# Strassen's seven products for a sample of two chunks, and prompt and sample in separate stages

## The chip, the cores and the metric

The kernel runs on one core of a Trainium2 chip. The metric is the device time of that core for one execution, in microseconds (us). The engines are named as the profile names them: PE is TensorE, which makes the matrix products, PEld its weight loads, DVE is VectorE, ACT is ScalarE, POOL is GpSimd, SP is SyncE, which issues the transfers. SBUF is the core's on-chip memory; PSUM is the memory into which PE writes.

## The reference

The program is a small encoder trunk of two layers with a width of 1024. It runs with the same weights on a prompt of 512 tokens and a sample of 1024 tokens. The core of it:

```python
for i in range(DEPTH):
    hn = rmsnorm(h, ln1[i])
    z = hn @ w_in[i]                        # 1024 -> 4352 columns
    q, k, v, ga, uf, gf, mga, mgf = jnp.split(z, SPLIT_IDX, axis=-1)
    ...
    a = band_attention(q, k, v, sink[i]) * jax.nn.silu(ga)
    f = fourier_mix(uf, w_fmix[i]) * jax.nn.silu(gf)
    merged = jax.nn.sigmoid(mga) * (a @ w_ao[i]) + jax.nn.sigmoid(mgf) * (f @ w_fo[i])
    h = h + merged @ w_out[i]
    gate = jax.nn.sigmoid(rmsnorm(h, ln_pg[i]) @ w_pg[i])
    h = h + (p[i].astype(h.dtype) @ w_pe[i]) * gate
return rmsnorm(h, ln_f)
```

`rmsnorm(x, g)` divides each token by the root of the mean of its squares and multiplies each channel by `g`. All of it is in float32.

## The kernel before

**Layout.** Channels lie on the 128 partitions and tokens on the free dimension. The 1536 tokens are three chunks of 512: chunk 0 is the prompt, chunks 1 and 2 are the sample. A width of 1024 is eight tiles k of 128 channels.

**Products.** A product of a 128x128 weight tile with a 128x512 activation tile is made in three passes: each operand is the exact sum of a hi and a lo half (`hi_lo`, L77: ACT casts to hi on L79, another engine subtracts to get lo on L80), and `mm3_steps` (L87) issues hi by hi (L91), hi by lo (L92) and lo by hi (L93). A result tile of 128 channels of one chunk has 8 k x 3 = 24 matmuls of 512 columns. `load_w` (L139) fetches a weight tile of eight k and splits it, ACT and POOL; the tile serves all three chunks, one after the other.

**Stages.** For each layer, `project` (L209) makes 34 tiles of the input projection for the three chunks. Beside it `run` interleaves, at so many steps per step of the projection, the input embedding's product, the attention (24 units: a block of 128 queries and one kv head), the Fourier mixing of the prompt and of the sample, and the first splits for the merge. Then `merge` (L301) has no second flow: both branches' projections with their gates, the output projection, and the gate's products (`w_pg`), each for eight tiles and three chunks. The residual h stays in SBUF through `merge`.

**Norm.** A token's scale is known only when all eight tiles of that token's h are there. `Norm.add` squares a tile on ACT and adds it on POOL (L182, L183); `stats` sums over partitions with tiny matmuls on PE (L188) and finds the reciprocal root with twelve tiny DVE operations (L190 to L197); `scale` spreads it over the partitions by transposes on PE (L203) and a copy (L205), and the result is the tile rb. The products do not wait for this: `split` (L165) puts only the channel's gain on a product's input, and rb is put on the product's output by DVE (`scaled`, L229; L354; for the rotary tables L249):

```python
def split(h, gain, k):
    t = big([P, 2, T], F32R)
    g = ln_sb[:, gain, k : k + 1]
    S.activation(t[:, 0, :], h, AF.Copy, scale=g)
    V.scalar_tensor_tensor(t[:, 1, :], h, g, f(t[:, 0, :]), op0=ALU.mult, op1=ALU.subtract)
```

**What sets the order.** The code is written for a tile framework: tiles come from pools with a fixed number of buffers (`BUFS`; PSUM has the tags mm, sc, o and misc with two banks each), the framework puts in the semaphores, and its scheduler puts each engine's instructions into an order when the program is built. At run time every engine works through its own list in that order.

## Time and profile before

| | |
|---|---|
| median of 3 runs | 2346.46 us (2344.33 to 2347.04) |
| the profiled execution, its span | 2344.3 us |
| mean granted TensorE clock | 0.988 |
| busy: PE, DVE, ACT, POOL | 97%, 51%, 34%, 28% |
| moved by DMA | 308.01 MB, 131 GB/s |

The span runs from the first to the last instruction of the profiled execution, which is one of its own beside the timed runs. In a row of the windows stand the stretch and its length, then busy time and number of instructions of PE, PEld, DVE, ACT and POOL, the granted clock (1.00 is full), the DMA engines' busy share and GB/s. A row of the timeline has start, duration, engine, line, operation, output and inputs by the program's names, and in brackets the idle time before it with what ended it. A row of the groups has the number of instructions, the busy sum, the mean ns of one, and the idle time before them. A matmul's duration is modelled and overlaps the next one.

### The profile page before, as it was taken

To read this page: it belongs to the slowest core of one execution; us is meant where nothing else is said; L and a number is where in the kernel's file an instruction comes from. 1 tells how busy PE (TensorE), PEld (TensorE's weight loads), DVE (VectorE), ACT (ScalarE), POOL (GpSimd) and SP (SyncE) were. 2 spreads that over 40 slices of the span, in tenths; PEclk is the share of its full clock that TensorE was granted. 3 is DMA by queue.
4 is the path that set the end of the run, shared out by engine and by line. 5 is a ranking of instruction groups with operands and counts; after the bars stand their busy time and mean duration, and the time that the engine had idled before them with its cause. 6 is when DMAs were issued, how large, how long until landed. Compare 5 with 4: busy or idle time off the path is not lost. (4 is left out here: it accounts for less than half of the span.)

```text
span 2344.3 us, 29343 instructions
## 1 busy us (share of the span) xinstructions
PE 2275.7 (97%) x10596; PEld 1885.0 (80%) x10596; DVE 1201.6 (51%) x2587; ACT 789.0 (34%) x1594; POOL 658.2 (28%) x427
## 2 busy tenths in 40 slices
...
GB/s 178 171 198 115 139 138 133 128 116 118 122 148 173 182 135 63 90 61 144 117 148 140 186 126 131 129 137 127 117 108 131 153 220 135 104 77 90 69 124 136
DMA packets 191905, 308.01 MB, mean 131 GB/s; under 512 B 15504, under 2 KB 89360, under 8 KB 191760
## 3 DMA queue, kind: packets, MB, share of 16 engines
...
HBM read 202.27 MB, written 103.81 MB: 131 GB/s over the span
## 5 line engine op out<-in xcount | busy, mean ns | idle before, releaser
L91 PE MATMUL mm<-act,wsp 128*128 128x512 f32 x1952 | 778.0, 399 | 2.6 <-DVE scr L222 2.6
L92 PE MATMUL mm<-act,wsp 128*128 128x512 f32 x1952 | 763.8, 391 | 1.2 <-DVE act L169 1.2
L93 PE MATMUL mm<-act,wsp 128*128 128x512 f32 x1952 | 763.4, 391 | 0.0
L80 POOL TENSOR_TENSOR wsp<-raw,wsp 128x1024 fp32r<-128x1024 f32 (+2 forms) x125 | 293.6, 2349 | 821.4 <-ACT wsp L79 671.2
L93 PEld LDWEIGHTS mm<-act,wsp 128*128 128x128 f32 x1952 | 366.8, 188 | 78.7
L91 PEld LDWEIGHTS mm<-act,wsp 128*128 128x128 f32 x1952 | 367.7, 188 | 69.9 <-issue 3.0
L92 PEld LDWEIGHTS mm<-act,wsp 128*128 128x128 f32 x1952 | 367.9, 188 | 69.3 <-DVE act L169 2.4
L79 ACT CAST wsp<-raw 128x1024 fp32r<-128x1024 f32 (+2 forms) x134 | 131.5, 986 | 427.0 <-PE mm L93 368.7
L229 DVE TENSOR_TENSOR scr<-mm,rb 128x512 f32<-128x512 f32 x170 | 117.3, 690 | 219.5 <-PE mm L93 218.2
L183 POOL TENSOR_TENSOR acc<-acc,scr 128x512 f32<-128x512 f32 x94 | 128.5, 1367 | 241.7 <-ACT scr L182 236.1
L501 ACT ACTIVATE act<-act,stat 128x384 f32<-128x384 f32 (+1 forms) x192 | 110.0, 574 | 199.4 <-DVE stat L499 198.5
L91 PE MATMUL sc<-act,wsp 128*128 128x512 f32 x416 | 165.9, 399 | 8.5 <-ACT act L168 8.5
L93 PE MATMUL sc<-act,wsp 128*128 128x512 f32 x416 | 165.2, 397 | 2.0 <-POOL wsp L80 2.0
L92 PE MATMUL sc<-act,wsp 128*128 128x512 f32 x416 | 165.7, 398 | 0.0
L91 PE MATMUL o<-act,wsp 128*128 128x512 f32 x416 | 163.2, 392 | 0.0
L92 PE MATMUL o<-act,wsp 128*128 128x512 f32 x416 | 162.6, 391 | 0.2 <-DVE act L169 0.2
L93 PE MATMUL o<-act,wsp 128*128 128x512 f32 x416 | 162.6, 391 | 0.0
L496 DVE CUSTOM_DVE_ANT_0 act<-sc,mask_sb 128x384 f32<-128x384 f32 (+1 forms) x192 | 91.1, 509 | 104.0 <-PE sc L491 103.5
L182 ACT ACTIVATE scr<-act 128x512 f32<-128x512 f32 x105 | 64.4, 628 | 227.6 <-DVE act L341 120.1
L80 DVE TENSOR_TENSOR act<-act,act 128x512 fp32r<-128x512 f32 (+1 forms) x144 | 113.3, 831 | 44.0 <-ACT act L79 40.6
L80 DVE TENSOR_TENSOR act<-misc,act 128x512 fp32r<-128x512 f32 x136 | 90.6, 686 | 52.0 <-ACT act L79 51.4
L323 POOL TENSOR_TENSOR act<-scr,scr 128x512 f32<-128x512 f32 x48 | 64.8, 1351 | 169.4 <-DVE scr L320 169.4
...
## 6 DMA issues: line engine op xcount, KB each, us to landing
...
gt<-scr SPq DMA_DIRECT2D x96, 256.0 KB, 2.0
scr<-gt SPq DMA_DIRECT2D x96, 256.0 KB, 2.8
q<-act SPq DMA_DIRECT2D x48, 256.0 KB, 3.2
gu<-scr SPq DMA_DIRECT2D x48, 256.0 KB, 2.2
pl<-scr SPq DMA_DIRECT2D x48, 256.0 KB, 2.2
...
```

Source lines behind the costliest of these rows:

```text
L79: S.copy(hi, src)
L80: lo_eng.tensor_tensor(lo, src, f(hi), op=ALU.subtract)
L91: PE.matmul(out, wh, xh, start=i == 0, stop=False)
L92: PE.matmul(out, wh, xl, start=False, stop=False)
L93: PE.matmul(out, wl, xh, start=False, stop=i == n - 1)
L182: S.activation(sq, h, AF.Square)
L183: eng.tensor_tensor(self.acc, self.acc, sq, op=ALU.add)
L229: V.tensor_tensor(a, out, rbs[c], op=ALU.mult)
L323: G.tensor_tensor(merged[c][-1][:, m % 2, :], ga, gf, op=ALU.add)
L496: V.tensor_tensor_reduce(out=pr, in0=sc[:, :W], in1=msk, scale=1.0, scalar=-3.0e38, op0=ALU.add, op1=ALU.max, accum_out=mx[:, e])
L501: S.activation(pr, pr, AF.Exp, bias=nmx[:, e], scale=0.125, accum_out=rs[:, e])
```

## The change

**Strassen's product.** For the sample, two weight tiles (m and m', 128 columns each), the two halves of the inner dimension (k 0 to 3, and 4 to 7) and the two chunks make a 2x2 by 2x2 block product. In place of eight half products of 4 k x 3 = 12 matmuls there are seven, in the form of Winograd with few sums. Class `Pair` holds it: four sums of weights on POOL, seven splits of weight halves (ACT, and POOL and DVE in turn), the seven products in three PSUM banks, and their combination by DVE and a copy by ACT. `pair_parts` makes the other side: for each k of the half, four differences on POOL and seven splits (ACT cast, DVE subtraction) of B11, T2, T1, T3, B21, T4, B22. This goes into the input projection (17 pairs of tiles), the output projection (4) and the gate (4). Both branches' projections of the sample keep plain products with weight tiles of half the depth.

**Stages.** Per layer they are now: A, the prompt's input projection (beside it the embedding, the prompt's attention and Fourier mixing, then the pair's parts); B, the pair's input projection; C, the prompt's whole merge (beside it the pair's 16 attention units and Fourier mixing, at 2.2 steps a step); D, both branches' projections of the pair; E, the pair's output projection; F, the pair's gate. Each weight is loaded and split once for the prompt and once for the pair. The pair's h goes to DRAM in E and is read again (`reload`) for F.

**Norm.** The scale rb is put on the inputs by DVE (`normed`, L287 of the changed kernel, called a scaling in the text; on L488 for the prompt's gate). The operations on the products' outputs (L229, L354 before) are gone, and the gates' tanh reads PSUM. At the start the prompt's scale is found first; in layer 0 the pair's squares are summed by POOL late in stage A (`first_pair`).

Comments are gone from the code, and the program is built with a smaller descriptor scratch (`dynamic_dma_scratch_size=256`).

```diff
-BUFS = dict(act=36, scr=9, raw=2, wsp=2, acc=3, rb=3, tiny=12, stat=20)
+PAIR = (1, 2)
+BUFS = dict(act=32, scr=9, raw=4, wt=4, wsp=9, acc=3, rb=3, tiny=12, stat=20)
...
+    class Pair:
+        ORDER = ("A11", "S2", "S1", "S3", "A12", "A22", "S4")
+        def __init__(self, src0, src1):
+            r0, r1 = (sbt([P, KD, P], F32, "raw") for _ in range(2))
+            SY.dma_start(r0, src0)
+            SY.dma_start(r1, src1)
+            self.a = dict(A11=r0[:, :4], A12=r0[:, 4:], A21=r1[:, :4], A22=r1[:, 4:])
+            self.w = {}
+        def prepare(self, i):
+            a, name = self.a, self.ORDER[i]
+            if i == 1:
+                for s in ("S1", "S2", "S3", "S4"):
+                    a[s] = sbt([P, 4, P], F32, "wt")
+                G.tensor_tensor(a["S1"], a["A21"], a["A22"], op=ALU.add)
+                G.tensor_tensor(a["S2"], a["S1"], a["A11"], op=ALU.subtract)
+                G.tensor_tensor(a["S3"], a["A11"], a["A21"], op=ALU.subtract)
+                G.tensor_tensor(a["S4"], a["A12"], a["S2"], op=ALU.subtract)
+            t = sbt([P, 2, 4, P], F32R, "wsp")
+            hi_lo(t[:, 0], t[:, 1], a[name], V if i % 2 else G)
+            self.w[name] = [(t[:, 0, k, :], t[:, 1, k, :]) for k in range(4)]
...
+        def steps(self, x, finish, following):
+            a, b, c = pst("mm"), pst("sc"), pst("o")
+            def product(bank, name, xs, first):
+                for k, ((wh, wl), (xh, xl)) in enumerate(zip(self.w[name], xs)):
+                    for n, (w, v) in enumerate(((wh, xh), (wh, xl), (wl, xh))):
+                        PE.matmul(bank, w, v, start=first and k == 0 and n == 0, stop=k == 3 and n == 2,
+                                  skip_group_check=True)
...
+            product(a, "A11", x["B11"], True)
+            s1 = scr()
+            S.copy(s1, a)
+            prepare(0)
+            yield
+            product(b, "S2", x["T2"], True)
+            q = scr()
+            V.tensor_tensor(q, b, s1, op=ALU.add)
+            prepare(1)
+            yield
+            product(c, "S1", x["T1"], True)
+            prepare(2)
+            yield
+            product(b, "S3", x["T3"], False)
+            v = scr()
+            V.tensor_tensor(v, b, s1, op=ALU.add)
+            prepare(3)
+            yield
+            product(a, "A12", x["B21"], False)
+            finish(0, 0, a, False)
+            V.tensor_tensor(v, c, v, op=ALU.add)
+            finish(1, 1, v, True)
+            prepare(4)
+            yield
+            product(b, "A22", x["T4"], False)
+            V.tensor_tensor(s1, b, s1, op=ALU.add)
+            finish(1, 0, s1, True)
+            prepare(5)
+            yield
+            product(c, "S4", x["B22"], False)
+            V.tensor_tensor(q, c, q, op=ALU.add)
+            finish(0, 1, q, True)
...
-    def split(h, gain, k):
-        t = big([P, 2, T], F32R)
-        g = ln_sb[:, gain, k : k + 1]
-        S.activation(t[:, 0, :], h, AF.Copy, scale=g)
-        V.scalar_tensor_tensor(t[:, 1, :], h, g, f(t[:, 0, :]), op0=ALU.mult, op1=ALU.subtract)
-        return t[:, 0, :], t[:, 1, :]
...
+    def normed(u, i, k, gain, rb):
+        V.scalar_tensor_tensor(u[:, i, :], u[:, i, :], ln_sb[:, gain, k : k + 1], rb, op0=ALU.mult, op1=ALU.mult)
+    def two(t):
+        return t[:, 0, :], t[:, 1, :]
+    def prompt_parts(us, gain, rb):
+        for k in range(KD):
+            normed(us[k // 2], k % 2, k, gain, rb)
+        return [two(halves(us[k // 2][:, k % 2, :], V)) for k in range(KD)]
+    def pair_parts(x, u1, u2):
+        t1, t2 = scr(), scr()
+        x["B11"].append(two(halves(u1[:, 0, :], V)))
+        G.tensor_tensor(t1, u1[:, 1, :], u1[:, 0, :], op=ALU.subtract)
+        G.tensor_tensor(t2, u2[:, 1, :], t1, op=ALU.subtract)
+        x["T2"].append(two(halves(t2, V)))
+        x["T1"].append(two(halves(t1, V)))
+        G.tensor_tensor(u1[:, 0, :], u2[:, 1, :], u1[:, 1, :], op=ALU.subtract)
+        x["T3"].append(two(halves(u1[:, 0, :], V)))
+        x["B21"].append(two(halves(u2[:, 0, :], V)))
+        G.tensor_tensor(u2[:, 0, :], u2[:, 0, :], t2, op=ALU.subtract)
+        x["T4"].append(two(halves(u2[:, 0, :], V)))
+        x["B22"].append(two(halves(u2[:, 1, :], V)))
+    def empty_pair():
+        return {n: [] for n in ("B11", "T2", "T1", "T3", "B21", "T4", "B22")}
+    def reload(k):
+        us = []
+        for kk in (k, k + 4):
+            u = big([P, 2, T])
+            for i, c in enumerate(PAIR):
+                SY.dma_start(u[:, i, :], H[c][kk])
+            us.append(u)
+        return us
+    def pair_normed(x, gain, rbs, source):
+        for k in range(4):
+            us = source(k)
+            for j in range(2):
+                for i in range(2):
+                    normed(us[j], i, k + 4 * j, gain, rbs[i])
+            yield
+            pair_parts(x, *us)
...
+    def project_pair(l, x, w, following):
+        p = Projection(l, PAIR)
+        for m in range(0, NMT, 2):
+            w_next = Pair(w_in[l, m + 2], w_in[l, m + 3]) if m + 2 < NMT else None
+            for _ in w.steps(x, lambda i, j, out, sb: p.finish(m + i, PAIR[j], out, sb), w_next):
                 tick()
-                if m == 0:
-                    norms[c].stats()
-                    after(2, lambda c=c, out=out: finish(0, c, out))
+                yield
+            w = w_next
+        handed.append(following())
...
+        norm.stats()
+        yield
+        yield
+        rb = norm.scale()
+        yield
+        xs = []
+        for k in range(KD):
+            u = scr()
+            V.scalar_tensor_tensor(u, hs[k // 2][:, k % 2, :], ln_sb[:, 2 + l, k : k + 1], rb, op0=ALU.mult, op1=ALU.mult)
+            xs.append(two(halves(u, V)))
+            yield
...
+            if h == 1 and i == 1:
+                pair_parts(x, part[j], part[j + 4])
...
+        for j in range(4):
+            w_next = Pair(w_out[l, j + 1], w_out[l, j + 5]) if j < 3 else Pair(w_pg[l, 0], w_pg[l, 4])
+            yield from w.steps(x, out_finish(j), w_next)
+            w = w_next
+        rbs = []
+        for n in norm:
+            n.stats()
+        for n in norm:
+            rbs.append(n.scale())
+        x = empty_pair()
+        yield from pair_normed(x, 2 + l, rbs, reload)
...
-            V.tensor_tensor(a, out, rb[c], op=ALU.mult)
...
+        S.activation(a, out, AF.Tanh, scale=0.5)
...
+    def first_pair(into):
+        us, ns = [], [Norm(), Norm()]
+        for k in range(4):
+            us.append([])
+            for kk in (k, k + 4):
+                u = big([P, 2, T])
+                for i, c in enumerate(PAIR):
+                    SY.dma_start(u[:, i, :], x[c, kk])
+                    ns[i].add(u[:, i, :])
+                us[-1].append(u)
+                yield
+        for n in ns:
+            n.stats()
+        yield
+        rbs = [n.scale() for n in ns]
+        yield
+        yield from pair_normed(into, 0, rbs, lambda k: us[k])
...
-        run(project(l, parts, norms, w), [
-            (embed(l), 4 * NCH * MT_GA, 1.2),
-            (attention(l), 4 * NCH * MT_U, RATE),
-            (chain(fourier(l, 0), fourier(l, 1), start_merge()), 4 * NCH * MT_U + FOURIER, RATE_F),
+        xs = empty_pair()
+        pair = first_pair(xs) if l == 0 else pair_normed(xs, 1, [norms[c] for c in PAIR], reload)
+        run(project_prompt(l, parts, w, lambda: Pair(w_in[l, 0], w_in[l, 1]).all()), [
+            (embed(l), 2, 1.0),
+            (attention(l, (0,)), 4 * MT_GA + 8, 1.2),
+            (chain(fourier(l, 0), pair), 4 * MT_GA + 80, 2.5),
         ])
-        parts, norms, w = merge(l, handed.pop())
+        run(project_pair(l, xs, handed.pop(), lambda: load_w(w_af[l, 0])), [
+            (start_merge_prompt(), 7 * (NMT // 2) - 3, 1.0),
+        ])
+        run(merge_prompt(l, handed.pop(), lambda: load_w(w_af[l, 0], G, (0,))), [
+            (chain(attention(l, PAIR), fourier(l, 1), start_merge_pair()), 0, 2.2),
+        ])
+        run(merge_pair(l, handed.pop(), (lambda: load_w(w_in[l + 1, 0])) if l + 1 < DEPTH else None), [])
+        if l + 1 < DEPTH:
+            w = handed.pop()
+            parts = next_parts()
```

In the programs' order, PE's instructions go from 10538 to 9938 (the 512-column matmuls with a weight tile from 8352 to 7752), DVE's from 2559 to 2896, ACT's from 1404 to 2020, POOL's from 432 to 1055, and SP's from 947 to 1194.

PE at the passage from the output projection to the gate in layer 0, before (mm, sc, o and misc are PSUM banks, acc the sums of squares):

```order
L92 MATMUL sc_8558<-act_8502,wsp_8384 128x512
L93 MATMUL sc_8558<-act_8502,wsp_8384 128x512
L188 MATMUL misc_8583<-mean_sb,acc_7722 128x1 x4
L91 MATMUL o_8603<-act_8505,wsp_8384 128x512
L92 MATMUL o_8603<-act_8505,wsp_8384 128x512
L93 MATMUL o_8603<-act_8505,wsp_8384 128x512
```

The first chunk's statistics stand there behind all 24 of its products of the first gate tile. The same passage of the pair in the change, on PE (L193 are the seven products; L266 and L281 are the statistics and the transposes):

```order
L193 MATMUL o_9648<-act_9170,wsp_9639 128x512 x3
L266 MATMUL misc_9799<-mean_sb,acc_9270 128x1 x4
L266 MATMUL misc_9819<-mean_sb,acc_9277 128x1 x4
L281 MATMUL misc_9839<-ident_sb,tiny_9805 128x128 x4
L193 MATMUL mm_10005<-act_9865,wsp_9663 128x512
L193 MATMUL mm_10177<-act_9865,wsp_10022 128x512
L193 MATMUL mm_10005<-act_9865,wsp_9663 128x512 x2
L281 MATMUL misc_9846<-ident_sb,tiny_9825 128x128 x4
L193 MATMUL mm_10177<-act_9865,wsp_10022 128x512 x2
L193 MATMUL sc_10006<-act_9870,wsp_9688 128x512
L193 MATMUL sc_10178<-act_9870,wsp_10047 128x512
L193 MATMUL o_10007<-act_9873,wsp_9703 128x512
```

Both chunks' statistics now stand ahead of the first gate product, and the products go by k, for two pairs of tiles at once. DVE of the change at that place (L283 is the copy that makes rb, L287 a scaling, L79 the subtraction for a lo half):

```order
L283 COPY rb_9851<-misc_9846 128x512
L287 SCALAR_TENSOR_TENSOR act_9853<-act_9853,ln_sb,rb_9851 128x512
L287 SCALAR_TENSOR_TENSOR act_9856<-act_9856,ln_sb,rb_9851 128x512
L79 TENSOR_TENSOR act_9870<-scr_9864,act_9870 128x512
L79 TENSOR_TENSOR act_9873<-scr_9863,act_9873 128x512
L79 TENSOR_TENSOR act_9877<-act_9853,act_9877 128x512
L79 TENSOR_TENSOR act_9880<-act_9856,act_9880 128x512
L79 TENSOR_TENSOR act_9884<-act_9856,act_9884 128x512
L79 TENSOR_TENSOR act_9887<-act_9856,act_9887 128x512
L287 SCALAR_TENSOR_TENSOR act_9890<-act_9890,ln_sb,rb_9844 128x512
L287 SCALAR_TENSOR_TENSOR act_9890<-act_9890,ln_sb,rb_9851 128x512
L79 TENSOR_TENSOR act_9902<-act_9890,act_9902 128x512
```

Before, DVE had one operation for each k and chunk there, the `split` of L169, and none of them read rb. POOL of the change in stage A of layer 0, where the pair's squares are summed (L261), weights split (L79) and summed (L176), and the first difference of `pair_parts` (L302) follows:

```order
L261 TENSOR_TENSOR acc_2677<-acc_2677,scr_2723 128x512
L261 TENSOR_TENSOR acc_2680<-acc_2680,scr_2727 128x512
L79 TENSOR_TENSOR wsp_3010<-wt_2990,wsp_3010 128x512
L261 TENSOR_TENSOR acc_2677<-acc_2677,scr_2732 128x512
L176 TENSOR_TENSOR wt_3086<-raw_3045,wt_3084 128x512
L261 TENSOR_TENSOR acc_2680<-acc_2680,scr_2736 128x512
L261 TENSOR_TENSOR acc_2677<-acc_2677,scr_2750 128x512
L261 TENSOR_TENSOR acc_2680<-acc_2680,scr_2754 128x512
L261 TENSOR_TENSOR acc_2677<-acc_2677,scr_2759 128x512
L261 TENSOR_TENSOR acc_2680<-acc_2680,scr_2763 128x512
L79 TENSOR_TENSOR wsp_3066<-raw_3045,wsp_3066 128x512
L302 TENSOR_TENSOR scr_2845<-act_2675 128x512
```

Before, the sums of chunks 1 and 2 stood on POOL at the program's start, beside the first products.

420 lines of the change are left out of this document (239 added, 181 removed).

## The prediction

> **What bounds the kernel now.** I read the page's head first, then windows of 25 us, then the timeline of TensorE.
>
> ```profile
> span 2344.3 us, 29343 instructions
> PE 2275.7 (97%) x10596; PEld 1885.0 (80%) x10596; DVE 1201.6 (51%) x2587; ACT 789.0 (34%) x1594; POOL 658.2 (28%) x427
> ```
> ```profile
> 0.00:25.00 25.00, 14.43 (x43) 10.55 (x44) 17.10 (x24) 20.84 (x35) 6.53 (x8) 0.93 0.81 295
> 1025.00:1050.00 25.00, 25.00 (x121) 20.89 (x120) 21.58 (x44) 12.15 (x21) 7.35 (x4) 1.00 0.10 32
> 1175.00:1200.00 25.00, 21.34 (x92) 17.19 (x91) 22.24 (x55) 4.99 (x7) 8.10 (x4) 0.86 0.35 107
> 300.00:480.00 180.00, 175.26 (x849) 144.30 (x848) 113.47 (x317) 75.63 (x186) 26.91 (x14) 0.99 0.42 131
> ```
> PE (first busy column) bounds nearly everything. The passage from the output projection to the gate's products, at 1025 to 1050, has PE full while DVE works 21.58 of 25 us: norm's statistics run beside the products. At the layer change (1175) little is lost. Only attention (300 to 480) leaves a steady 4.74 us of 180 empty, 2.6%.
>
> A matmul's modelled 0.39 us is not its price; starts are closer:
>
> ```profile
> 1079.65 0.39 PE L93 MATMUL mm<-act,wsp 128*128 128x512 f32 x1
> 1121.81 0.39 PE L93 MATMUL sc<-act,wsp 128*128 128x512 f32 x1
> 10.29 0.63 PE L91 MATMUL sc<-act,wsp 128*128 128x512 f32 x1
> 10.71 0.63 PE L92 MATMUL sc<-act,wsp 128*128 128x512 f32 x1
> ```
> The first two are 186 matmuls apart: 42.16 / 186 = **0.2267 us** each. The last two are cold: 0.42 apart just after the start.
>
> **What it removes.** Matmuls of 512 columns with a weight tile go from 8352 to 7752 in the programs' order: 600 x 0.2267 = **136 us** off PE's stream (not 600 x 0.39 = 234). All other PE work stays. Done by half, the gain is 68; since the count is certain, I take all of it.
>
> **What it adds** is work on DVE, ACT and POOL (337, 616 and 623 instructions more), and places where PE must wait for it. Prices:
>
> ```profile
> L80 DVE TENSOR_TENSOR act<-act,act 128x512 fp32r<-128x512 f32 x128 | 107.3, 883 | 43.4 <-ACT act L79 40.1 <-DMA pl<-scr 2.9
> L358 DVE SCALAR_TENSOR_TENSOR act<-scr,act 128x512 f32<-128x512 f32 x48 | 33.2, 691 | 1.4
> L183 POOL TENSOR_TENSOR acc<-acc,scr 128x512 f32<-128x512 f32 x94 | 128.5, 1367 | 241.7 <-ACT scr L182 236.1 <-PE misc L188 4.7
> L79 ACT CAST act<-act 128x512 fp32r<-128x512 f32 x144 | 80.5, 618 | 41.3 <-POOL act L323 13.7 <-DMA act<-in_w_pe 9.6 <-DVE act L80 6.4
> L182 ACT ACTIVATE scr<-act 128x512 f32<-128x512 f32 x105 | 64.4, 628 | 227.6 <-DVE act L341 120.1 <-DVE act L358 102.9 <-DVE tiny L196 2.8
> ```
> DVE's price depends on POOL:
>
> ```profile
> 8.46 5.62 DVE L169 SCALAR_TENSOR_TENSOR act<-act,ln_sb,act 128x512 fp32r<-128x512 f32 x8
> 20.56 8.49 DVE L169 SCALAR_TENSOR_TENSOR act<-act,ln_sb,act 128x512 fp32r<-128x512 f32 x8
> 23.35 21.31 POOL L183 TENSOR_TENSOR acc<-acc,scr 128x512 f32<-128x512 f32 x14 [3.26 <-ACT scr L182]
> ```
> Eight take 5.62 us (0.70 each) with POOL idle and 8.49 (1.06 each) beside POOL's adds, which then need 1.52. The change puts POOL beside DVE at every boundary (pair_parts alternates them), so I take the upper price there and keep 0.70 as the lower bound.
>
> The Trainium skill, "SBUF — State Buffer", section "Who interferes with whom", says that a DVE instruction with two SBUF inputs and a reading GpSimd instruction exclude each other wholly. By the rule a k of the pair's parts would cost as in the third rival below. The rows show a slowing of both, milder than that: 8 x 0.70 of DVE inside 8.49 us, during which POOL finished five and a half adds.
>
> The statistics' chain stands in the tail:
>
> ```profile
> 2322.72 0.39 PE L93 MATMUL mm<-act,wsp 128*128 128x512 f32 x1
> 2328.25 1.84 PE L188 MATMUL misc<-mean_sb,acc 128*128 128x1 f32 x8 [5.14 <-DVE acc L183]
> 2330.13 0.16 DVE L190 TENSOR_SCALAR tiny<-misc 128x4 f32<-128x4 f32 x1 [2.02 <-PE misc L188]
> 2332.30 0.16 DVE L197 SCALAR_TENSOR_TENSOR tiny<-tiny,tiny 128x4 f32<-128x4 f32 x1
> 2333.74 0.69 DVE L205 COPY rb<-misc 128x512 f32<-128x512 f32 x1 [1.27 <-PE misc L203]
> 2334.46 6.07 DVE L371 SCALAR_TENSOR_TENSOR scr<-act,ln_sb,rb 128x512 f32<-128x512 f32 x6
> 2334.56 3.44 POOL L369 TENSOR_TENSOR scr<-act,rb 128x512 f32<-128x512 f32 x2 [18.19 <-issue]
> ```
> From the last product's end (2323.1) to the scale rb (2334.4) it is 11.3 us. Before, PE met this once, at the end, because the scale went on the products' outputs. With the scale on inputs, no product of the next stage starts before rb. Stage by stage:
>
> *Output projection to gate, sample pair (E to F), twice.* Both chunks' statistics stand on PE ahead of the first gate product. 11.3 us for one chunk, about 3 for the second (2.3 of small DVE ops, a copy): rb at 15. All gate products are queued behind these statistics on PE, and DVE's combinations wait for those in turn. The first k needs scalings, two POOL differences, casts and subtractions, all parts complete at about 26. Each further k costs DVE 4 x 1.01 + 7 x 0.88 = 10.2 us, so k=2 is done at 46, and the B11 part of k=3, which the first product needs to end, at 49.5. In between PE has only the products on k=0 to 2 that its order lists, about 45 matmuls = 10.2 us. Gap 49.5 - 10.2 - 2 (parts that start before k is complete) = **37**, with a colder clock +1. With DVE uncontended (0.69 each, 7.6 per k) about 29.
>
> *Prompt projection to pair projection (A to B).* Layer 0 has the x statistics of two chunks: 14 POOL adds at 1.37 and some four more POOL ops, 24 us, begun only with the 31st of 34 prompt tiles; then small ops and the same chain of k. It ends 54 to 63 us after that tile, and PE has 3 tiles x 24 x 0.2267 = 16.3, plus 10.2 of early products: **33** (28 to 37; 25 uncontended). Layer 1 has its scale already and two k done early: **10** (6 to 15).
>
> *Prompt merge with the pair's attention (C), twice.* The attention's rows:
>
> ```profile
> L496 DVE CUSTOM_DVE_ANT_0 act<-sc,mask_sb 128x384 f32<-128x384 f32 x128 | 66.2, 553 | 78.1 <-PE sc L491 78.0
> L496 DVE CUSTOM_DVE_ANT_0 act<-sc,mask_sb 128x256 f32<-128x256 f32 x64 | 24.9, 420 | 25.9 <-PE sc L491 25.6
> L80 DVE TENSOR_TENSOR act<-misc,act 128x512 fp32r<-128x512 f32 x136 | 90.6, 686 | 52.0 <-ACT act L79 51.4
> L509 DVE TENSOR_SCALAR act<-act,stat 128x384 f32<-128x384 f32 x128 | 45.1, 416 | 1.1
> L509 DVE TENSOR_SCALAR act<-act,stat 128x256 f32<-128x256 f32 x64 | 18.3, 350 | 0.6
> L499 DVE SCALAR_TENSOR_TENSOR stat<-stat,nsink_sb 128x1 f32<-128x1 f32 x192 | 34.7, 199 | 0.1
> L544 DVE TENSOR_TENSOR scr<-o,scr 64x512 f32<-64x512 f32 x24 | 16.7, 695 | 8.9 <-ACT scr L542 8.4
> L543 DVE TENSOR_TENSOR scr<-o,scr 64x512 f32<-64x512 f32 x24 | 16.2, 676 | 7.5 <-ACT scr L541 7.5
> L504 DVE TENSOR_TENSOR stat<-sink_sb,stat 128x4 f32<-128x4 f32 x48 | 16.3, 339 | 1.5
> L532 PE MATMUL o<-act,act 128*128 128x512 f32 x256 | 87.0, 408 | 9.9 <-ACT act L79 4.6 <-DVE act L80 4.5
> L527 PE MATMUL misc<-ident_sb,act 128*128 128x128 f32 x512 | 76.2, 273 | 0.0
> L491 PE MATMUL sc<-act,act 128*128 128x384 f32 x256 | 55.8, 338 | 0.0
> L491 PE MATMUL sc<-act,act 128*128 128x256 f32 x128 | 22.5, 289 | 2.7 <-DVE stat L496 2.7
> ```
> Over 48 units these are 329.0 / 48 = 6.9 us of DVE and 241.5 / 48 = 5.0 of PE a unit; with smaller groups, under 16 us each, I estimate DVE at 7.2. Sixteen units and the prompt's 384 matmuls are 16 x 5.0 + 384 x 0.2267 = 167 us of PE against 16 x 7.2 + 23 (24 combinations x 0.69, 8 subtractions x 0.84) = 138 of DVE: 83% against 63% in the 300-to-480 row, in chains of five dependent steps. Between 2.6% (4) and a wait of 1.7 us a unit (27), I take 16, nearer the middle since no row has this density. Then the prompt's own gate products: rb (11), 8 scalings x 1.01, 8 subtractions x 0.84 and the Fourier pieces among them, 38 us on DVE against 22.8 of Fourier work for PE: 15, and 5 in Fourier's own chains. Together **36** a layer (14 to 60).
>
> H's way through DRAM, KB each and us to landing:
>
> ```profile
> h<-act SPq DMA_DIRECT2D x24, 256.0 KB, 2.0
> scr<-h SPq DMA_DIRECT2D x24, 256.0 KB, 4.0
> ```
> *Smaller.* Start: the prompt's norm now comes ahead of its first product. Its adds end at about 13 (estimated from the loads behind the 8.46 row), statistics to rb take 6.2 (2328.25 to 2334.4), eight scalings 5.6, cast and subtraction 1.4: first product at 26 instead of 8.5. Before, PE idles or runs cold for about 24 in all (43 matmuls in the first 25 us); now 26 + 5 cold: **+7** (4 to 10). Last part of the pair's merge (D to E): one pair_parts is left after the last product, two scalings, a POOL sum 1.37, cast, subtraction, and a weight behind six POOL ops: **5** twice (1 to 10). Layer change: the next prompt's scalings queue with the pair's last combinations on DVE: **4** (0 to 8); the 1175 row loses as much already. Tail: two chunks' results, 12 x 1.01 on DVE instead of 6, **+6** (3 to 9). Small waits in A, B, E on ACT copies and banks: **10**. Weights are loaded and split twice, H is read again on SP's queue behind its own writes: at 0.42 DMA share (300-to-480 row) I cost that at nothing. The re-read of k=0's tiles follows writes a whole pair of products older, that of k=3 has the 30 us of scaling before it as cover; without it, a write and a read are some 6 us, twice.
>
> The Trainium skill, "TensorE: Matmul & The Clock Gate", section "Why this matters for your kernels", says that a TensorE gap of over about 3 us drops the clock to half. Granted clock 0.86 in the 1175 row and 0.42 us spacing after the start agree. By the rule each of some eight boundary gaps would add 2 to 3 us, about 18 beyond the sum, except that bursts there wait for the next k anyway.
>
> **Sum**, against the profiled span: 2344.3 - 136 + 7 (start) + 43 (A to B) + 72 (C) - 28 (attention's and Fourier's present stalls: 2.6% of about 1090 us) + 10 (D to E) + 76 (E to F) + 4 + 6 + 10 = **2408**. The runs' median lies 2 us over that span: **2410**, 2.7% slower.
>
> **The rivals.**
> 1. *Faster: POOL does not slow DVE and PE's cover suffices.* Where POOL waits for DVE and not beside it, as in the 8.46 row, all ops cost 0.70. Place: the boundaries; lower bounds: start +4, A to B 31, C 28 - 28, D to E 2, E to F 58, others 15: 2344 - 136 + 110 = 2318. It decides once all added waiting stays below 136. For it: attention before loses just 2.6%. Against: the 20.56 row, and the chain of statistics that no price of DVE removes. Chance 0.12.
> 2. *Much slower: DVE bounds C.* If each unit waits 3 us and the prompt's gate waits 40: 2 x (48 + 20 - 36) = +64: 2474. For it: 83% with dependent steps, and POOL doubling its work. Against: 97% PE beside attention now. Chance 0.17.
> 3. *DVE and POOL exclude each other wholly.* A k with 4 scalings, 7 subtractions and 4 differences then takes 11 x 0.70 + 4 x 1.37 = 13.2 us instead of 10.2. At three k's of two E to F and one A to B that is +27, and I put as much on the other boundaries and the tail by half: +40: 2450. For it: both slow in the 20.56 and 23.35 rows. Against: eight scalings there lost 2.9 us, not the 7.7 of 5.6 adds. It is the mechanism of the first page named above. Chance 0.07.
> 4. *No change:* waiting of 131 to 141 happens to cancel the gain: 2344. Chance 0.04.
> 5. That the change does not do what it says is out: the 600 matmuls are gone from the order.
>
> **How the numbers follow.** The forecast (2375 to 2445) has 0.60. The range of 2350 to 2475 holds it, the exclusion and most of the second rival. What a measurement of this kernel can tell from no change is about 0.2%. Faster 0.12 (rival 1), same 0.04 (rival 4), slower 0.84.
>
> **What would show it.** PE's stream: 7752 matmuls still 0.2267 apart. In the waits of PE, the largest groups must be the first products of the gate stage, on the lo parts of DVE (about 37 us each, twice), then one of about 33 at the first pair product, and DVE scalings at 1.0 us there. In C, PE's gaps must end by DVE's attention lines. If PE's share stays above 93%, I am wrong on the boundaries; if it falls below 85%, C is worse than priced. If the scalings take 0.70, contention was overpriced.

## The result and the profile after

The change makes the kernel **16.3% slower**: a median of 2727.85 us (2725.9 to 2729.93) against 2345.42 (2344.33 to 2347.04), a ratio of 1.163 [1.161, 1.164]. The prediction had the direction, but gave +64 us for what is +382. The page's head of the kernel after:

```profile
span 2728.1 us, 30370 instructions
PE 2310.8 (85%) x9996; PEld 1855.6 (68%) x9996; DVE 1576.8 (58%) x2924; ACT 1077.0 (39%) x2210; POOL 1398.0 (51%) x1050
```

The 600 matmuls are gone (10596 before, 9996 now). Yet PE's busy time rose by 35 us, because a busy row of PE is a modelled time, which is longer where the clock is low (0.63 us in the cold rows of the prediction, 0.39 in the others); the mean granted clock fell from 0.988 to 0.910. So the span is lost in two ways: PE waits, and runs slowly between its waits. Windows of the kernel after, with the columns as before (PE, PEld, DVE, ACT, POOL, clock, DMA share, GB/s):

```profile
525.00:550.00 25.00, 25.00 (x112) 20.70 (x111) 9.86 (x14) 8.84 (x15) 14.15 (x12) 1.00 0.29 98
715.00:990.00 275.00, 239.44 (x1168) 191.62 (x1167) 225.22 (x542) 146.46 (x354) 126.41 (x96) 0.95 0.52 171
1225.00:1250.00 25.00, 14.77 (x34) 9.47 (x33) 14.11 (x21) 6.34 (x12) 10.99 (x8) 0.57 0.12 44
1250.00:1275.00 25.00, 14.92 (x31) 9.21 (x31) 18.07 (x21) 10.28 (x18) 13.03 (x9) 0.57 0.00 0
```

In the middle of stage B (525) the seven products run at full rate: 112 matmuls in 25 us. In the passage E to F (1225 to 1275) PE gets through 65 instructions in 50 us, where some 220 matmuls of 512 columns would fit (50 / 0.2267), and **no engine is full**: DVE is busy for 32 of the 50 us, POOL for 24. That is the mark of a chain that goes round between engines. PE's largest waits in the kernel after (total, times, longest):

```profile
PE misc L266 <- POOL acc L261: 60.2, 12, 7.3
PE sc L193 <- ACT act L78: 50.5, 15, 11.8
PE mm L193 <- ACT scr L202: 40.6, 10, 8.5
PE sc L193 <- DVE scr L207: 33.5, 9, 6.9
PE mm L193 <- ACT act L78: 30.0, 11, 3.7
PE o L744 <- DVE act L79: 26.8, 24, 2.1
PE mm L193 <- DVE scr L540: 20.8, 2, 10.4
```

No single wait is as long as the 37 us that were predicted; behind the start PE waits often, for up to 12 us, and for all three of the other engines. Statistics wait for POOL's sums (L266), products for parts (L78), and, which the prediction had not looked for, the later products of a pair for the reading of its earlier ones: the fourth product goes on in the second's bank, which the first combination (L207) must have read before, and the fifth in the first's bank, which a copy (L202) must have read before.

In stage B this costs time in the first four pairs alone (windows of layer 0, then one such wait on DVE and PE):

```profile
392.00:462.00 70.00, 56.69 (x226) 45.49 (x225) 51.99 (x70) 18.64 (x33) 45.18 (x31) 0.88 0.48 136
462.00:715.00 253.00, 253.00 (x1118) 209.50 (x1117) 89.84 (x127) 96.50 (x163) 135.46 (x102) 1.00 0.40 131
426.89 1.74 DVE L351 TENSOR_TENSOR scr<-scr,scr 128x512 f32<-128x512 f32 x1 [1.15 <-POOL scr L350]
428.55 0.68 DVE L207 TENSOR_TENSOR scr<-sc,scr 128x512 f32<-128x512 f32 x1
429.28 4.45 PE L193 MATMUL sc<-act,wsp 128*128 128x512 f32 x12 [6.78 <-DVE scr L207]
```

The first three pairs are the tiles of K, V and Q. Their rotary tables are work for DVE and POOL in turn (L348 to L351), and the next pair's L207 stands behind it on DVE. From 462 on, over 13 pairs, PE has no gap and the full clock; layer 1 is the same.

To place the loss I cut both traces into stages by counting matmuls, and took from each stage's length its PE instructions, each at its median spacing in the trace of before (0.2267 us for one of 512 columns). What is left is waiting, slow clock and the ends of chains, to some 10 us over the whole. Before lost 106 us in all. The rows with plain products are explained below.

| loss in us, both layers | A | B | C | D | E | F | tail | all |
|---|---|---|---|---|---|---|---|---|
| after | 111 | 111 | 128 | 28 | 72 | 151 | 34 | 635 |
| plain products, scale on inputs | 92 | 4 | 127 | 27 | 14 | 25 | 28 | 317 |
| plain products, scale on outputs | 76 | 8 | 104 | 31 | 17 | -1 | 27 | 262 |

### The profile page after: what moved, and what is told of

It is laid out like the page before. It is cut to its first block, busy times and chain, and to the rows that moved or that the text cites. A ratio compares the mean times of both kernels' runs of the same rounds, so it can differ in the third digit from the quotient of the medians.

```text
span 2728.1 us, 30370 instructions
## 1 busy us (share of the span) xinstructions
PE 2310.8 (85%) x9996; PEld 1855.6 (68%) x9996; DVE 1576.8 (58%) x2924; ACT 1077.0 (39%) x2210; POOL 1398.0 (51%) x1050
## 5 line engine op out<-in xcount | busy, mean ns | idle before, releaser
L79 POOL TENSOR_TENSOR wsp<-raw,wsp 128x512 fp32r<-128x512 f32 x348 | 474.1, 1365 | 551.7 <-ACT wsp L78 511.3
L193 PE MATMUL sc<-act,wsp 128*128 128x512 f32 x1800 | 487.2, 419 | 99.4 <-ACT act L78 50.5
L193 PEld LDWEIGHTS sc<-act,wsp 128*128 128x128 f32 x1800 | 363.2, 204 | 197.5 <-ACT act L78 59.8
L78 ACT CAST wsp<-raw 128x512 fp32r<-128x512 f32 x414 | 255.4, 619 | 487.3 <-PE sc L193 150.2
L193 PE MATMUL mm<-act,wsp 128*128 128x512 f32 x1200 | 326.9, 419 | 98.5 <-ACT scr L202 40.6
L90 PE MATMUL mm<-act,wsp 128*128 128x512 f32 x936 | 385.7, 413 | 28.9 <-ACT scr L401 11.7
L91 PE MATMUL mm<-act,wsp 128*128 128x512 f32 x936 | 378.7, 405 | 1.8 <-DVE act L79 1.0
L92 PE MATMUL mm<-act,wsp 128*128 128x512 f32 x936 | 375.6, 402 | 0.0
L193 PEld LDWEIGHTS mm<-act,wsp 128*128 128x128 f32 x1200 | 240.5, 203 | 165.3 <-ACT scr L202 46.0
L193 PE MATMUL o<-act,wsp 128*128 128x512 f32 x1200 | 306.2, 402 | 0.6 <-DVE act L79 0.6
L193 PEld LDWEIGHTS o<-act,wsp 128*128 128x128 f32 x1200 | 233.7, 195 | 52.9 <-DVE act L79 3.0
L79 POOL TENSOR_TENSOR wsp<-wt,wsp 128x512 fp32r<-128x512 f32 x100 | 137.1, 1371 | 219.4 <-ACT wsp L78 215.8
L79 DVE TENSOR_TENSOR act<-act,act 128x512 fp32r<-128x512 f32 (+1 forms) x248 | 209.3, 880 | 60.5 <-ACT act L78 58.2
L90 PEld LDWEIGHTS mm<-act,wsp 128*128 128x128 f32 x936 | 182.3, 195 | 64.9 <-ACT scr L401 12.8
L78 ACT CAST act<-act 128x512 fp32r<-128x512 f32 (+2 forms) x272 | 149.2, 594 | 161.3 <-POOL act L309 56.6
L92 PEld LDWEIGHTS mm<-act,wsp 128*128 128x128 f32 x936 | 181.6, 194 | 38.5
L91 PEld LDWEIGHTS mm<-act,wsp 128*128 128x128 f32 x936 | 183.0, 195 | 35.4 <-DVE act L79 4.5
L261 POOL TENSOR_TENSOR acc<-acc,scr 128x512 f32<-128x512 f32 x98 | 132.4, 1356 | 129.8 <-ACT scr L260 122.4
L78 ACT CAST wsp<-wt 128x512 fp32r<-128x512 f32 x200 | 122.6, 619 | 158.9 <-PE sc L193 54.7
L79 DVE TENSOR_TENSOR act<-scr,act 128x512 fp32r<-128x512 f32 (+1 forms) x126 | 124.4, 1005 | 91.0 <-ACT act L78 90.1
L78 ACT CAST act<-scr 128x512 fp32r<-128x512 f32 (+1 forms) x126 | 72.1, 591 | 244.8 <-POOL scr L303 134.8
```

The lines of the kernel that those rows point to most:

```text
L78: S.copy(hi, src)
L79: lo_eng.tensor_tensor(lo, src, f(hi), op=ALU.subtract)
L90: PE.matmul(out, wh, xh, start=i == 0, stop=False)
L91: PE.matmul(out, wh, xl, start=False, stop=False)
L92: PE.matmul(out, wl, xh, start=False, stop=i == n - 1)
L193: PE.matmul(bank, w, v, start=first and k == 0 and n == 0, stop=k == 3 and n == 2, skip_group_check=True)
```

## The experiments

In the expectations N is the theory that the scale on the inputs costs the time, S that the seven products do (their parts and their combination). R says that reads come late for want of a scratch buffer, K that the chain of one k's parts sets E to F, X that DVE and POOL shut each other out, D that DVE's amount of work decides, and B that the last k's parts bound the passage from A to B. All times stand against runs of before on the same chip (medians 2345.2 to 2347.4).

### Which part of the change costs the time

**Seven products undone**: plain products for the pair, as eight half products; the scale stays on the inputs.

```diff
-        ORDER = ("A11", "S2", "S1", "S3", "A12", "A22", "S4")
+        ORDER = ("A11", "A12", "A21", "A22")
...
+            for n, (i, j) in enumerate(((0, 0), (0, 1), (1, 0), (1, 1))):
+                out = mm_ps()
+                mm3(out, self.w[f"A{i + 1}1"] + self.w[f"A{i + 1}2"], x[f"B1{j + 1}"] + x[f"B2{j + 1}"])
+                finish(i, j, out, False)
```

> The pair's three products (input projection, output projection, gate) are made with eight half products again, four splits of each k in place of seven and no sums on POOL; stages and the norm's scale on the inputs stay as in the change. PE's stream gets the 600 matmuls back: +136 us. Theory N (the waits come from the scale on the inputs): boundaries stay, only the parts of each k get cheaper (about 30 us in all), so about 2728 + 136 - 30 = 2830. Theory S (Strassen's own combinations hold PE up: each product waits for a copy or a sum of the one before, 164 us lost inside the pair's stages of the change): the loss inside these stages nearly vanishes and the boundaries get cheaper, about 2728 + 136 - 164 - 60 = 2640, faster than the change.

Measured 2555.21 us, 1.089 [1.087, 1.090].

**Scale put back on the outputs**: the seven products stay.

```diff
-        V.scalar_tensor_tensor(u[:, i, :], u[:, i, :], ln_sb[:, gain, k : k + 1], rb, op0=ALU.mult, op1=ALU.mult)
+        S.activation(u[:, i, :], u[:, i, :], AF.Copy, scale=ln_sb[:, gain, k : k + 1])
...
-        yield from pair_normed(x, 2 + l, rbs, reload)
+        yield from pair_normed(x, 2 + l, reload)
...
+        V.tensor_tensor(a, out, rb, op=ALU.mult)
+        S.activation(a, a, AF.Tanh, scale=0.5)
```

> Seven products and stages stay; the scale goes on the products' outputs again, as in the kernel before (gain by ACT on the inputs, one DVE multiplication for each result, scaled rotary tables). Theory N: the start, both passages from prompt to pair and both from output projection to gate no longer wait for the statistics: of some 250 us lost there about 200 come back, 2728 - 200 = 2530. Theory S: what holds PE up are the combinations and the making of seven parts for each k, which stay, with one DVE operation more for each result: 2660 to 2720.

Measured 2681.7 us, 1.142 [1.139, 1.145].

**Both undone**, so that only the separate stages are left (the two edits above together).

> Both undone: plain products and scale on the outputs, in the separate stages. What is left against the kernel before (2345) is the price of the stages alone: weights loaded and split twice, attention of the pair beside the prompt's merge, h through DRAM. If the stages cost nothing by themselves, 2345 to 2370; if the crowded merge stage of the prompt costs what the change's trace shows there (65 us lost in each layer against about 20 before), about 2345 + 90 + 30 = 2465.

Measured 2496.72 us, 1.064 [1.062, 1.065].

The three give a ladder: before 2345; the stages alone 2497 (**+151**); the scale on the inputs 2555 (**+58**); the seven products 2728 (**+173**). N falls: the scale that the prediction made responsible costs 58 under plain products and 46 (2728 less 2682) under the seven. S stands, and had put even 85 us too little on them (2640 for 2555): the seven products save 136 us of PE work and cost about 309 of waiting. The table says where: with plain products B, E and F lose 43 us together, with the seven 334. The same passage under plain products and scale on inputs, windows of that run:

```profile
1175.00:1200.00 25.00, 17.94 (x71) 13.10 (x72) 21.98 (x51) 8.17 (x14) 0.71 (x1) 0.86 0.59 211
1200.00:1225.00 25.00, 25.00 (x111) 20.57 (x110) 23.11 (x33) 14.19 (x26) 7.03 (x4) 1.00 0.59 186
1194.53 0.50 PE L90 MATMUL sc<-act,wsp 128*128 128x512 f32 x1 [0.76 <-ACT act L78]
```

POOL has one operation in the first stretch, DVE is nearly full, and PE is full from the second on: here the scale costs one short gap. A k now needs only four scalings and four subtractions, in the trace 5.2 us of DVE (1187.90 to 1193.08), and lets PE issue 18 matmuls (4.1 us) in the three banks that are open: PE waits less than 1 us for each k (the 1194 row), and with the last one it has whole products to make.

### Late reads

**No reads of the old h** in E, and none of h and of the embedding's product in F; the sums with them are left out too.

```diff
-                SY.dma_start(old, x_in[c, m] if l == 0 else H[c][m])
-                V.scalar_tensor_tensor(old, out, 0.25, old, op0=ALU.mult, op1=ALU.add)
+                V.tensor_scalar(old, out, 0.25, None, op0=ALU.mult)
...
-                SY.dma_start(pl, PL[c][m])
...
-                SY.dma_start(h, H[c][m])
-                gate_out(out, in_sbuf, pl, h)
```

> The change, with the reads of the old h in the pair's output projection and of h and the embedding's part in the pair's gate left out (h is 0.25 times the product, and 0.5 times the gate's value plus 0.5; the sums are not made), so that no result waits for a transfer or for the buffer that it goes into. Theory R (the ring of nine scratch buffers makes these reads late, and PE's copies and sums queue behind them on DVE and ACT): the output projection and gate stages lose 112 us now and would lose about 45: 2660. Theory S (the order of the combinations themselves): 2710 to 2730.

Measured 2653.12 us, 1.130 [1.129, 1.132]: 75 us less.

**The same reads into other buffers**: nothing left out, the tiles come from the large pool (`act`) in place of the nine scratch buffers (in the last layer's gate the embedding's product stays where it was).

```diff
-                old = scr()
+                old = big([P, 2, T])[:, 0, :]
...
+                    both = big([P, 2, T])
+                    pl = both[:, 0, :]
...
-                    h = scr()
+                    h = both[:, 1, :]
```

> The change, with the reads of the old h (output projection of the pair, both layers) and of h and the embedding's part (gate of the pair, first layer) put into the large buffers instead of the nine scratch buffers, so that they can be issued earlier; nothing is left out. Without these reads the kernel took 2653, 75 less. Theory R (they come late for want of a scratch buffer): most of that, 2670 or less. Theory L (it is the transfer itself, or the order in SP's queue): 2710 to 2730.

Measured 2665.05 us, 1.136 [1.134, 1.138]: 63 us less. So of the 75 us that the reads cost, 63 come from the nine buffers, not from bytes. (The reads get a buffer sooner, and other tiles that use the nine do too; the run does not separate the two.) Stage F of the kernel after shows it (timeline, SP, DVE, ACT and PE):

```profile
1326.69 0.33 SPq L590 DMA_DIRECT2D h<-scr  x1
1327.07 0.42 SPq L578 DMA_DIRECT2D scr<-pl  x1
1327.54 0.44 SPq L586 DMA_DIRECT2D scr<-h  x1
1329.95 1.25 DVE L431 SCALAR_TENSOR_TENSOR scr<-scr,scr 128x512 f32<-128x512 f32 x1 [0.42 <-DMA scr<-pl]
1332.35 0.69 DVE L432 SCALAR_TENSOR_TENSOR scr<-scr,scr 128x512 f32<-128x512 f32 x1 [1.14 <-DMA scr<-h]
1333.13 0.63 ACT L260 ACTIVATE scr<-scr 128x512 f32<-128x512 f32 x1 [5.30 <-DVE scr L432]
1333.67 0.57 ACT L202 COPY scr<-mm 128x512 f32<-128x512 f32 x1
1334.29 0.79 PE L193 MATMUL mm<-act,wsp 128*128 128x512 f32 x1 [8.53 <-ACT scr L202]
```

Read it from the top. The reads go out only right behind the store of an earlier tile (1326.69); that of h lands late; DVE's sum waits for it; ACT's square (L260) waits 5.30 us for the sum; and the copy L202, which needs none of this, stands behind the square in ACT's fixed order. PE waits 8.53 us for the bank. In the run with the other buffers the group "PE mm L193 <- ACT scr L202" falls from 40.6 us to 12.4; "PE sc L193 <- DVE scr L207", which has most of its waits in B, stays at 32.5. In E of the kernel after, DVE stood idle before L555, the sum with the old h, until these reads landed (us and times; in the run with the other buffers it never did):

```profile
  DMA scr<-in_x: 22.0, 11
  DMA scr<-h: 20.4, 11
```

At the end of E this hits the statistics (timeline of the kernel after):

```profile
1210.54 0.38 SPq L554 DMA_DIRECT2D scr<-in_x  x1
1212.26 1.87 PE L266 MATMUL misc<-mean_sb,acc 128*128 128x1 f32 x8 [7.31 <-POOL acc L261]
1216.42 0.69 DVE L555 SCALAR_TENSOR_TENSOR scr<-scr,scr 128x512 f32<-128x512 f32 x1
1219.27 1.86 PE L266 MATMUL misc<-mean_sb,acc 128*128 128x1 f32 x8 [5.15 <-POOL acc L261]
1227.59 0.69 DVE L283 COPY rb<-misc 128x512 f32<-128x512 f32 x1 [2.00 <-PE misc L281]
```

The last product of E ends at 1205 (1212.26 less 7.31). The second chunk's last sum is read for only at 1210.54, then stands on DVE behind the first chunk's twelve tiny operations (until 1216.4), and its scale is there at 1228.3, 23 us after the product; the prediction had 15.

### The parts of a k

**F uses E's parts**: the pair's second norm and the second making of parts are left out.

```diff
-                norm[ci].add(old)
...
-        x = empty_pair()
-        yield from pair_normed(x, 2 + l, rbs, reload)
```

> The change, with the pair's second norm left out: the gate's products read the parts of the output projection's input again, so that no statistics, scalings, re-read or parts stand between the two stages; everything within the stages stays. Theory K (the passage is long since each k costs DVE some 10 us and only three of the seven products can start before the last k): the gate stage, 154 us now, falls to about 100 in each layer, 2728 - 108 = 2620. Theory S (the chain of combinations inside the stage): it falls by the statistics alone, some 15 in each layer, 2700.

Measured 2568.11 us, 1.096 [1.093, 1.098]: 160 us less, more than K had said. E and F lose some 66 us in place of 223. The stretch around the former passage in this run:

```profile
1175.00:1200.00 25.00, 25.00 (x112) 20.68 (x112) 10.32 (x14) 7.02 (x12) 15.76 (x12) 1.00 0.39 137
1200.00:1225.00 25.00, 22.08 (x92) 17.77 (x91) 14.69 (x16) 9.37 (x17) 15.27 (x11) 0.94 0.47 168
```

F's reads of h are still there in this run, from the nine buffers, and F loses only some 20. So they are late only behind the passage, where the products of two pairs run together and eight results want buffers at once; that step is argued, not shown. The costs of the reads and of the passage therefore overlap and may not be added.

One k's parts in the kernel after, DVE and POOL (timeline):

```profile
1241.12 2.42 DVE L287 SCALAR_TENSOR_TENSOR act<-act,ln_sb,rb 128x512 f32<-128x512 f32 x2
1245.63 1.69 DVE L79 TENSOR_TENSOR act<-scr,act 128x512 fp32r<-128x512 f32 x2 [2.08 <-ACT act L78]
1250.62 1.29 DVE L79 TENSOR_TENSOR act<-act,act 128x512 fp32r<-128x512 f32 x2 [2.10 <-ACT act L78]
1240.57 1.77 POOL L302 TENSOR_TENSOR scr<-act 128x512 f32<-128x512 f32 x1 [3.38 <-DVE act L287]
1243.68 1.26 POOL L303 TENSOR_TENSOR scr<-act,scr 128x512 f32<-128x512 f32 x1 [1.34 <-issue]
1248.67 1.27 POOL L309 TENSOR_TENSOR act<-act,scr 128x512 f32<-128x512 f32 x1 [2.50 <-DVE act L79]
1253.32 1.77 POOL L302 TENSOR_TENSOR scr<-act 128x512 f32<-128x512 f32 x1 [3.38 <-DVE act L287]
```

From one first difference to the next (1240.57 to 1253.32) it is **12.7 us**, against the predicted 10.2. DVE's own work in it is less than predicted, 8.6; what was missing is two waits of 2.1 us in which DVE stands idle. The second difference on POOL (L303) waits for the last scaling, ACT casts it, and only then has DVE something to subtract; likewise the last one (L309). In the fixed order nothing of the next k may fill that time.

**All four differences on DVE**, k by k as before.

```diff
-        G.tensor_tensor(t1, u1[:, 1, :], u1[:, 0, :], op=ALU.subtract)
-        G.tensor_tensor(t2, u2[:, 1, :], t1, op=ALU.subtract)
+        V.tensor_tensor(t1, u1[:, 1, :], u1[:, 0, :], op=ALU.subtract)
+        V.tensor_tensor(t2, u2[:, 1, :], t1, op=ALU.subtract)
...
-        G.tensor_tensor(u2[:, 0, :], u2[:, 0, :], t2, op=ALU.subtract)
+        V.tensor_tensor(u2[:, 0, :], u2[:, 0, :], t2, op=ALU.subtract)
```

> The change as it is, k by k, with only pair_parts' four differences on DVE instead of POOL, at every passage. In the change's trace a k takes 12.7 us at the gate's passage, in which DVE idles for 4.2: it is a chain from DVE to POOL to ACT to DVE. Without POOL in it a k is 15 x 0.70 = 10.5 on DVE plus what is left of waiting for the casts, about 11.5. Theory X: four passages of three to four k's gain 1 to 2 us a k, and the passage of the merge one POOL sum, 2690 to 2715. Theory D: 2740.

Measured 2673.44 us, 1.140 [1.138, 1.142]: 54 us less, though DVE has four operations a k more. Two successive k in this run, DVE:

```profile
1229.39 1.41 DVE L287 SCALAR_TENSOR_TENSOR act<-act,ln_sb,rb 128x512 f32<-128x512 f32 x2
1239.96 1.41 DVE L287 SCALAR_TENSOR_TENSOR act<-act,ln_sb,rb 128x512 f32<-128x512 f32 x2
```

A k takes 10.6 us, nearly all of it work: 15 operations at 0.69 are 10.35. DVE doing everything alone is faster than DVE and POOL taking turns.

**F's parts made part by part** (all scalings and B11 first, then T2 of all k, and so on), so that PE could begin whole products early; the differences once on POOL, once on DVE.

```diff
-        yield from pair_normed(x, 2 + l, rbs, reload)
+        us = [reload(k) for k in range(4)]
+        for k in range(4):
+            for j in range(2):
+                for i in range(2):
+                    normed(us[k][j], i, k + 4 * j, 2 + l, rbs[i])
+                    if i + j == 0:
+                        x["B11"].append(two(halves(us[k][0][:, 0, :], V)))
+        t1s = []
+        for u1, u2 in us:
+            t1s.append(scr())
+            G.tensor_tensor(t1s[-1], u1[:, 1, :], u1[:, 0, :], op=ALU.subtract)
...
```

> The change, with the pair's parts for the gate made part by part (B11 of all four k first, then T2, T1, T3, B21, T4, B22) instead of k by k. The instructions are the same; only their order on DVE, POOL and PE changes. Theory K: a product can then start as soon as its own four splits are made, PE runs beside DVE from the first part on (28 splits and 16 scalings of about 0.9 are 41 us, two pairs of tiles are 38 of PE): the gate stage falls by some 30 in each layer, 2670. Theory S: no change beyond 10 us.

> The change, with the parts for the gate made part by part and their sixteen differences on DVE instead of POOL. Part by part alone gave 2714: its trace shows scalings of 1.69 us each beside POOL's differences of 1.7, and 0.74 without. Theory X (a DVE operation with two SBUF inputs and a POOL operation exclude each other): without POOL the 60 operations of a passage are 60 x 0.72 = 43 us, PE runs along after the first eight, and the gate stage falls from 152 to about 115 in each layer, 2640. Theory D (DVE's own amount of work sets the passage): sixteen more operations on DVE are 11 us more in each layer, 2735.

Measured 2713.63 us, 1.157 [1.154, 1.159], with POOL, and 2702.0, 1.152 [1.150, 1.153], with DVE. Both gain little (14 and 26 us), where K and X had given 2670 and 2640. The scalings of the two runs, with POOL beside them and without (timelines, first run DVE and POOL, second run DVE):

```profile
1236.61 10.13 DVE L287 SCALAR_TENSOR_TENSOR act<-act,ln_sb,rb 128x512 f32<-128x512 f32 x6
1237.90 1.59 POOL L581 TENSOR_TENSOR act<-act,scr 128x512 f32<-128x512 f32 x1
1239.45 1.71 POOL L586 TENSOR_TENSOR act<-act,act 128x512 f32<-128x512 f32 x1
```
```profile
1233.99 4.06 DVE L287 SCALAR_TENSOR_TENSOR act<-act,ln_sb,rb 128x512 f32<-128x512 f32 x6
```

Six scalings take 10.13 us beside POOL, 1.69 each, and 4.06 without, 0.68 each. So X's price of a scaling is right, but not the gain that it gave. By the starts of PE's matmuls, the loss up to the gate's fifth product falls with DVE from 49 us in each layer to 31 and 30, 38 in all, but about 12 come back inside the pairs behind it. All sixteen scalings now stand ahead of the second product's parts; that this keeps the gain in the passage small is argued from the order, not shown.

**The last k's parts for B left out** (k=2's taken twice).

```diff
-    def pair_normed(x, gain, rbs, source):
+    def pair_normed(x, gain, rbs, source, n=4):
...
-        for k in range(4):
+        for k in range(n):
...
+        for v in x.values():
+            v += v[-1:] * (4 - n)
```

> The change, with the last k of the pair's parts for the input projection left out (the parts of k=2 stand in for those of k=3), at the gate nothing changed. 37 large buffers would be needed to have all 28 parts beside the prompt's eight and its table, and there are 32; with three k it is 30. Theory B (the fourth k's parts wait for buffers that only the prompt's last products free): both passages from prompt to pair shrink by more than the one k, from some 55 and 45 us lost to about 25 and 10, 2660 to 2670. Theory K (each k costs the same): one k of 12.7 in each, 2703.

Measured 2712.86 us, 1.157 [1.155, 1.159]: 15 us less. B falls, and K's 25 was too much: the passage from A to B isn't bound by the buffers of the last k.

### Clock and attention

**PE kept warm**: twelve further matmuls for each k into a spare bank, whose result nothing reads.

```diff
+            wh, keep = x["B11"][k][0], pst("misc")
+            for _ in range(12):
+                PE.matmul(keep, wh[:, :P], wh, start=True, stop=True)
```

> The change, with twelve products of 512 columns more on PE behind each k's parts, into a spare bank that nobody reads, in the stretches where PE waits for DVE. They keep PE from idling so long that its granted clock halves (0.57 there now). If the halved clock costs time there and behind it (26 us of slowed matmuls in each gate stage, 15 in each of the pair's projections), 2728 - 40 = 2690 or less; if these matmuls wait for the next k anyway, as the prediction held, 2725 to 2735; if the added products are in the way, more.

Measured 2726.16 us, 1.162 [1.160, 1.164]: no change. The same two stretches in this run:

```profile
1225.00:1250.00 25.00, 15.95 (x52) 11.04 (x50) 15.00 (x21) 7.46 (x13) 11.10 (x8) 0.87 0.05 19
1250.00:1275.00 25.00, 18.62 (x59) 13.48 (x60) 17.12 (x22) 9.39 (x17) 12.55 (x10) 0.80 0.11 32
```

The granted clock there goes from 0.57 to 0.87 and 0.80, and the time stays: products that wait for the next k lose nothing by being slow.

**Attention without the division by the sum.**

```diff
-            for i, pr in enumerate(probs):
-                V.tensor_scalar_mul(pr, pr, rd[:, i : i + 1])
```

> The change, with the division of the attention's probabilities by their sum left out (four DVE operations of 0.51 to 0.58 in each of 48 units). If DVE's amount of work bounds the prompt's merge with the pair's attention (67 and 61 us lost there), its 64 operations there are 36 us less for each of the two stages, and 2728 - 2 x 30 = 2670; if the losses there come from the order of the steps, or from the norm and Fourier parts, 2715 or more.

Measured 2687.2 us, 1.146 [1.144, 1.147]: 41 us less, between the two. Stage C gets shorter by only 11 and 15 us in the two layers. Some 16 more come in A and the passage behind it, where the prompt's eight units of a layer lose the same operations, which the expectation had not counted. DVE's busy time in C falls from 227 and 226 us to 201 and 196; PE's instructions there fill 214 at full rate. So DVE had some 13 us more to do than PE, and about that much is gained. What the other 50 us of C wait for is not settled.

### Remedies together, and whether any pays

**Other buffers, differences on DVE, parts by part** in one kernel (the three edits above).

> The change with all three edits: the reads of h into large buffers, pair_parts' differences on DVE, the gate's parts part by part. If they are separate causes that add up: 2728 - 63 - 55 - 15 = 2595. If they hide one another (the chain of one product on the other remains): 2640 or more. Plain products took 2555 in these stages.

Measured 2615.2 us, 1.115 [1.112, 1.118]: 113 us less; alone the three gave 63, 54 and 14 (26 with DVE), so they mostly add up.

**Scale on outputs, other buffers, differences on DVE.**

> Seven products, scale on the outputs (2682 so far), with the reads of h into large buffers and the differences on DVE. If the causes add up: 2682 - 63 - 55 = 2564; plain products with the scale on the outputs took 2497. If the seven products pay once the waits are gone it would have to come below 2497.

Measured 2588.46 us, 1.104 [1.101, 1.106]: 93 us less than 2682, of the 118 that the two gave alone, and 92 above plain products without any of these remedies.

**The same, with seven products only in the pair's input projection** and plain ones in E and F.

```diff
+    class Plain:
+        ORDER = ("A11", "A12", "A21", "A22")
...
+            for n, (i, j) in enumerate(((0, 0), (0, 1), (1, 0), (1, 1))):
+                out = mm_ps()
+                mm3(out, self.w[f"A{i + 1}1"] + self.w[f"A{i + 1}2"], x[f"B1{j + 1}"] + x[f"B2{j + 1}"])
+                finish(i, j, out, False)
```

> Seven products in the input projection of the pair alone (17 pairs of tiles, 408 of the 600 matmuls, 92 us), plain products in its output projection and gate; scale on the outputs, differences on DVE, reads of h into large buffers. Against plain products everywhere (2497) it saves 92 on PE and loses what the passage from prompt to pair costs more with 28 parts than with 16: with scale on the outputs that was 127 us, less some 29 for POOL. If this holds: 2497 - 92 + 98 = 2503, even. If the passage hides behind the prompt's last products: 2420.

Measured 2513.51 us, 1.071 [1.069, 1.074]. Plain products everywhere had 2496.72. The projection is the longest stage, with 17 pairs of tiles on one set of parts; it saves 2 x 17 x 12 x 0.2267 = 92 us of PE there, and even that does not come out ahead. Its first four pairs still lose 21 and 29 us in the two layers, as in the kernel after, and the 13 behind them nothing. These 50 us are more than the 17 that it lacks, so with the rotary work out of L207's way the projection alone might pay against 2497; no run tests that. No version that I ran beats the kernel before.

## Why the prediction was right in direction and wrong in size

Its sum took off 136 and added 200 us. The added loss is near 520 (384 of span and the 136), 320 more. By its own steps:

- **The 600 matmuls, 136 us, not 234: right.** The count is exact and steady stages run at full rate (the 525 and 462 rows).
- **Start, first product at 26: right**, as PE's timeline of the kernel after has it:

```profile
25.52 0.79 PE L90 MATMUL sc<-act,wsp 128*128 128x512 f32 x1 [2.22 <-ACT act L78]
```

- **"Small waits in A, B, E on ACT copies and banks: 10": the step that failed most.** Inside the pairs of tiles, after a stage has got going, B loses 26 us in each layer, E 25 and 27, F 32 and 28: 164. The prediction took a pair's seven products as a block that PE runs through, and priced only the ways into a stage. F stands in no such term at all. In truth the fourth and fifth product of a pair wait for a copy and a sum, which stand in the fixed order of ACT and DVE behind other work: in B behind the rotary tables of the first pairs (the 428 row), in E mainly, and in F in part, behind late reads and squares (the 1333 rows). With the reads in other buffers E loses only 10 us a layer inside its pairs. Plain products meet the same work and do not wait for it: each goes into a fresh bank (B loses 4 us with them in all).
- **"H is read again ... I cost that at nothing": wrong, 63 to 75 us**, some of it the same as in the point above. The reason given was the DMA engines' share of 0.42. Bandwidth was not the limit; the read could not be issued for want of one of nine buffers, and every in-order queue behind it waited too.
- **E to F, 37 twice (76 with the colder clock): mis-sized, 49 twice**, 22 us more. (With F's pairs that is 7 more than the table has for F, whose last products stand beside the next prompt's first.) Two terms were short: the scales came 23 us after the last product, not 15, and a k took 12.7, not 10.2. The k was not longer for dearer operations: DVE worked 8.6 us in it and stood for 4.2.
- **The contended price of 1.06: misread.** It was the mean of eight operations, half of which ran before POOL began. A narrower window of the same trace of before separates them:

```profile
20.56 3.39 DVE L169 SCALAR_TENSOR_TENSOR act<-act,ln_sb,act 128x512 fp32r<-128x512 f32 x5
23.21 5.84 DVE L169 SCALAR_TENSOR_TENSOR act<-act,ln_sb,act 128x512 fp32r<-128x512 f32 x4
23.35 6.86 POOL L183 TENSOR_TENSOR acc<-acc,scr 128x512 f32<-128x512 f32 x4 [3.26 <-ACT scr L182]
```

  The first five take 0.68 each, the last four 1.46, beside POOL's adds at 1.72. The rival that POOL and DVE exclude each other was therefore nearer the truth than its 0.07; its "against" used the same average, and counted five and a half adds of POOL where some three fit between 23.35 and 29.05. (The two rows of DVE come from windows that share an operation.)
- **A to B, 33 and 10: mis-sized, 57 and 36.** The prediction counts from the end of the 31st prompt tile; from there to the pair's fifth product PE loses 57 and 36 us by its starts, 93 for 43. The table by stages puts part of it into A: in layer 0 PE waits 7.2 us there for a copy (L401), and 7.1 for POOL's sums of the pair's squares (L266), before the last prompt tiles are through. Plain products lose nearly as much in A (64 and 28, after 70 and 41, with the start in the first).
- **C, 36 a layer: mis-sized, 67 and 61.** The prediction had DVE at 83% of PE's work for the attention and the branches' projections. In the whole stage DVE is busy for 227 us (225.22 in the 715 row), and PE's instructions fill 214: DVE had more to do than PE. The second rival put 68 there, for the reason of a full DVE; by the run without the division that holds for some 13 of it, and the rest is open.
- **D to E, 5 twice: 10.4 twice**, at the upper end of its range. The rows of the kernel after:

```profile
1097.97 1.69 DVE L79 TENSOR_TENSOR act<-scr,act 128x512 fp32r<-128x512 f32 x2 [7.34 <-ACT act L78]
1101.61 3.56 PE L193 MATMUL mm<-act,wsp 128*128 128x512 f32 x8 [10.40 <-DVE scr L540]
1096.02 1.26 POOL L303 TENSOR_TENSOR scr<-act,scr 128x512 f32<-128x512 f32 x1
```

  DVE stands for 7.34 us until POOL, behind sums and weight splits, reaches the second difference at 1096.02. The queue on POOL was in the step; that the combination which frees PE's bank (L540) stands on DVE behind the same wait was not.
- **Tail, +6: +13.** 34 us behind the last product (2728.1 less 2694.3), where before had 21 (2344.3 less 2323.1).
- **Cold clock, no cost beyond the sum: right.** The Trainium skill, "TensorE: Matmul & The Clock Gate", section "Why this matters for your kernels", says to leave no gap of over about 3 us; the rows agree that such gaps halve the clock (0.57, with gaps of PE of up to 4.8 us in the two stretches), and the warm run shows that ending this gains nothing where PE isn't what is waited for.
- **Attribution: wrong.** The text put the loss on the scale that stands before the first product of a stage. Undoing the scale gives back 46 us, undoing the seven products 173.

So the passages, on which the prediction spent nearly all its work, were too low by a fifth to a little over a half, but for the start; the pairs' own waits, set at 10, make about half of the miss (154 of 320). Of its signs, the two waits of 37 us before the gate did not appear as such, and PE's share came out at the lower bound that it named (85%).

Left open: the rest of the loss at A to B (differences on DVE gave some 19 us there, one k less 15), what C waits for beyond DVE's excess, and how the 151 us of the separate stages divide further, beyond the table's last row (A 76 with the start, C 104, D 31).
